# A two-layer hybrid decoder step: recurrence pace, place of the decode update, and how the output projections get their inputs

## The chip, the core and the metric

One NeuronCore of a Trainium2 chip runs the whole program. The engines work side by side, each through its own queue in order: TensorE (PE, with its weight loads PEld), VectorE (DVE), ScalarE (ACT), GpSimd (POOL) and SyncE (SP), which here only issues DMA transfers. The metric is the device time of one execution in microseconds; lower is better.

## The reference

The step takes 1024 new prompt tokens behind 16 meta tokens and 8 single decode tokens through two layers of width 1024. Layer 0 is a Conformer convolution and an MLP, layer 1 is RWKV-7 time mixing and an MLP. What matters here is layer 1:

```python
def _wkv7_step(S, inp):
    r_t, w_t, k_t, v_t, kk_t, a_t = inp
    sa = jnp.einsum('bhvk,bhk->bhv', S, -kk_t)
    S = (S * w_t[:, :, None, :] + sa[..., None] * (kk_t * a_t)[:, :, None, :]
         + v_t[..., None] * k_t[:, :, None, :])
    y = jnp.einsum('bhvk,bhk->bhv', S, r_t)
    return S, y
...
    kk = kk / jnp.maximum(jnp.sqrt(jnp.sum(kk * kk, axis=-1, keepdims=True)), L2_EPS)
...
    S_final, ys = lax.scan(_wkv7_step, S0.astype(f32), xs)
...
    out = ((yn + bonus).astype(h.dtype) * g) @ w_o
    return out, h[:, -1], S_final.astype(S0.dtype)

def _sqrelu_mlp(h, w_in, w_out):
    return jnp.square(jax.nn.relu(h @ w_in)) @ w_out
```

There are 16 heads of 64, the MLP is 4096 wide, and `yn` is the head-wise normalised `y`. The scan runs over 1040 prompt tokens; the decode tokens make one step each from a state of their own.

## The kernel before

**Groups, chunks and stages.** Features lie on the 128 partitions as 8 tiles (`KT`), tokens along the free dimension. Layer 0 runs over three groups of tokens. The time mixing (`mixer_in`) runs over four groups `G1` of 256 to 272 tokens: for each of 8 feature blocks p it projects r and v (8 matmuls each), and for the next group the keys (`keys`), and makes from them the operands `ab` of the recurrence, written to memory as `d_ab`. The recurrence works on 17 chunks: chunk 0 is the meta tokens, and each group gives four chunks of 64 tokens (group 0 gives chunks 0 to 4, and group 3 gives 13 to 16). The output projection (`mixer_out`, 24 matmuls for each of 8 output blocks) and the MLP of layer 1 run over three groups `G2` of 328 and 352 tokens: group 0 by itself, then groups 1 and 2 together. Their products are three matmuls each, of a high and a low part of weights and inputs (`split`, `load_w`); GpSimd makes the low parts of the weights (`wi_lo`, `wo_lo`).

**The recurrence.** A chunk needs the inverse of a triangular matrix for each head. `inverses` makes it for all chunks of a group at once on VectorE: 30 steps of two instructions (`tt`, `ni`), each needing the one before, then a store to `d_p`. `front(c)` loads a chunk's operands, makes the products `A` in two halves, masks them into `xa` and `nr`, and transposes the inverse `p32` in blocks into `x32`. `chunk(c)` goes on with the products gg (from x32), bT, W, po, U, S and Y in this order; the results pass through VectorE and ScalarE (`w1`, `p64`, `uv`, `fs`, `sv`). Chunk c+1 needs the state `sv` of chunk c.

**What sets the order.** TensorE executes the mixer and the first group's output projection and MLP in the order in which the program yields them (`manual_schedule`); a scheduler orders the other engines' instructions by when they could run and by program order. `recurrence` is a generator that yields a weight after each step (`RW`, 27.7 a chunk). In the mixer `tick` runs 7 times for a feature block or so: it makes a step of the inverse, gives the recurrence a credit of `PACE[g]` and lets it run until the credit is used. In the MLP of group 0 `fill`, made by `filler`, does the same at 208 points: over all of them it takes a stated weight from each of several streams, here the recurrence, the decode update and the normalisation of y (`norm_gate`, tiles ey, ems, eq, ez), whose result `d_z` is what the output projection reads.

**The decode update.** `decode_step` brings the decode operands into place through four transposes (`pdd`) and then updates the 8 x 16 decode states in 16 slices of 128x256 (`Sdec`, `t4`, printed as t in the profile): a load, nine VectorE instructions and a store each, with two buffers. The last normalisation unit waits for it.

**The output projection's inputs.** `mixer_out` loads each of the 8 input tiles `zr` by a transfer of its own into a three-deep scratch buffer, splits it into `z`, and loads and splits the weights `wo` of an output block where that block begins. The MLP's inputs `m_h` and `m_l` take the places of `z`, so they wait for the last reads of it; the products' sums of squares come from the matmul `st_m`.

Of the kernel before, what the change touches and what calls it, by code (L numbers as in the profile page):

```python
# [8 lines left out]
F32 = mybir.dt.float32  # L9
# [7 lines left out]
P = 128  # L17
D = 1024
KT = D // P
# [16 lines left out]
N2 = 352  # L36
# [12 lines left out]
def hybrid_step(tc, x_prompt, x_sample, state_conv, state_shift, state_wkv, meta_tokens,  # L49
# [8 lines left out]
    nc = tc.nc  # L58
    ctx = ExitStack()
    with ctx:  # L60
# [61 lines left out]

        def open_tmp(stack, nmax, tag, bufs=3, **kw):
            cur["n"] = cur["wide"] = nmax
            cur["tmp"] = pool(stack, f"tmp{tag}", bufs, **kw)
            cur["stat"] = pool(stack, f"stat{tag}", 1, **kw)

# [741 lines left out]
        def keys(g, fill):  # L869
# [10 lines left out]
            for p in range(KT):  # L880
                yield
                ps = proj(next(wrkv), act, n, nm("k", p), fill)
                k_ = kept[g, p] = pr.tile([P, N1], F32, name=nm("st", p), tag="st", bufs=KT + 1)
                nc.scalar.copy(k_[:, :n], ps[:, :n])
                sq = pr.tile([P, N1], F32, name=nm("sq", p), tag="rk", bufs=2)
                nc.scalar.activation(sq[:, :n], ps[:, :n], AF.Square, scale=vec("k_k", p))
                add_pn()
                add_pn = to_pn(p, sq)
            r16 = lorap.tile([P, N1], F32, name=nm("r16"), tag="lf")
            r16p = norm[g] = [lorap.tile([P, N1], F32R, name=nm("r16" + q), tag="r16" + q, bufs=2)[:, :n] for q in "hl"]  # L890
# [7 lines left out]
        def mixer_in(g, tick):  # L898
# [75 lines left out]
            act_v = mixed(3)  # L974
            r16p = norm.pop(g)
            ks = iter(())

# [54 lines left out]
            for p in range(KT):  # L1032
                both()
                ps = proj(next(wrkv), act, n, nm("r", p), both)
                rk2 = pr.tile([P, 2, N1], F32, name=nm("rk2", p), tag="rk2", bufs=2)
# [23 lines left out]
                pb = bank(nm("pb", p))  # L1059
                spread(pb[:, :n], r16p, p)  # L1060
                nc.vector.scalar_tensor_tensor(nkk[:, :n], kp[:, :n], nvec("k_k", p), pb[:, :n], op0=ALU.mult, op1=ALU.mult)
# [39 lines left out]
                if g < 3:  # L1101
                    if p == 0:
                        for _ in ranked(PP, prepare(g + 1)):
                            pass
                        ks = keys(g + 1, both)
                        next(ks)
                    for _ in keys_of(p):
                        next(ks, None)
# [49 lines left out]
        def front(c):  # L1158
# [10 lines left out]
            nc.sync.dma_start(p32, d_p[c].rearrange("k r t -> r k t"))  # L1169
            yield RW[0]  # L1170
            mask = lambda x: m_ar[:, x].unsqueeze(1).broadcast_to([P, 4, HS])
            for j in range(0, KT, 4):
# [14 lines left out]
                if j == 0:  # L1187
                    yield RW[1]
            x32 = w_([P, KT, 32], "x32", c)
            nc.vector.transpose(flat(x32), flat(p32))  # L1190
            chunks[c] = xa, bk, nr, no, p32, x32
# [262 lines left out]
        ng0 = norm_gates(GN_OF[0])  # L1454
        PACE = [0, 2.0, 2.0, 2.0]

# [7 lines left out]
        with in_order():  # L1464
            shift_in()
            for _ in prepare(0):
                pass
            for _ in keys(0, lambda: None):
                pass
            for g in range(4):  # L1470
                mixer_in(g, lambda slow=1.0: tick(g, slow))
            carry["tail"]()
            while invert():
                pass
            advance(CHUNK_WAIT * NCH, NEED[GN_OF[0][-1]])
            for _ in ng0:
                pass
        ld.close()


        with ExitStack() as l1:
            open_tmp(l1, N2, "2", 3)
            actp = pool(l1, "actp1", 1)
            open_weights(l1, 0, {"w": 5}, "f")
            residp = pool(l1, "resid1", 1)
# [6 lines left out]
            def mixer_out(g, residp, actp, fill, add):  # L1492
                lo, n = G2[g]
                h1 = hl[g] = residp.tile([P, KT, cur["wide"]], F32, name=f"h1_{g}", tag="h")
                nc.sync.dma_start(h1[:, :, :n], d_h[:, :, lo:lo + n])
                z = new_acts(actp, f"z{g}", cur["wide"])
                for p in range(KT):
                    t = tt(f"zr{g}{p}", "t1")
                    nc.sync.dma_start(t[:, :n], d_z[:, p, lo:lo + n])
                    split(z[0][p][:, :n], z[1][p][:, :n], t[:, :n], nc.vector)  # L1500
                for m in range(KT):
                    ps = dense(load_col(rwkv_w_o[0], m, f"wo{g}_{m}", nc.gpsimd), z, n, f"oo{g}_{m}", fill)
                    nc.vector.tensor_add(h1[:, m, :n], h1[:, m, :n], ps[:, :n])
                    add(m, h1[:, m, :n])
                    fill()
# [57 lines left out]
            def group(g, actp, hidp, sums):  # L1563
# [3 lines left out]


            ng2 = norm_gates(GN_OF[2])
            fill, rest = filler(2 * KT + MLP_POINTS,  # L1570
                                ([until(NCH - 1)], FA * CHUNK_WAIT * (NCH - 1 - st["done"])),
                                ([decode_step()], 82), ([norm_gates(GN_OF[1]), ng2], NGA))
            add, sums = sums_of(0)
# [63 lines left out]
```

## Time and profile before

| | |
|---|---|
| time, median of 3 runs | 2803.23 us (2798.64 to 2806.42) |
| the profiled execution: its own time | 2803.45 us |
| its span, first to last instruction | 2801.7 us |
| TensorE busy | 2654.4 us (95%) |
| VectorE, ScalarE, GpSimd busy | 63%, 41%, 53% |
| granted TensorE clock, mean | 0.977 |
| mixer from its second group on, MLP of group 0 up to its block 16 | 1310 to 1827.5 us, 1899.7 to 2097 us |

All times count from the span's start. A row of the windows view gives for a stretch the busy time and the number of instructions of each engine, then the granted clock, the DMA share and GB/s. A row of groups gives line, engine, operation, tiles and shapes with its count, then busy time and mean duration in ns, then the idle time before and what ended it. A row of waits gives who waited for whom, the total in us, how often, and the longest. A row of the timeline gives start and duration in us. Tile names stand without their numbers there.

### The profile page before, as it was taken

The numbers are of one execution on the slowest core, as the hardware profiler recorded it, in microseconds if no ns is written. First come the engines' busy times: TensorE is split into PE (matmuls) and PEld (weight loads), VectorE is DVE, ScalarE is ACT, GpSimd is POOL, SyncE is SP. The second block draws the span as 40 slices with busy tenths as digits, with TensorE's granted clock in tenths as the row PEclk, the third lists the DMA queues.
The fourth block names the chain that finished last, engine by engine and source line by source line (L and its number), as shares of the span: only waits on it lengthen the run. The fifth ranks groups of instructions, "written<-read, shape, count | busy, mean of one in ns | idle before, by whom it ended". The sixth has DMA issues, their size and how long they took to land. (4 is left out here: it accounts for less than half of the span.)

```text
span 2801.7 us, 51779 instructions
## 1 busy us (share of the span) xinstructions
PE 2654.4 (95%) x19866; PEld 2502.9 (89%) x19866; DVE 1772.9 (63%) x3550; ACT 1141.9 (41%) x2101; POOL 1497.7 (53%) x2066
## 2 busy tenths in 40 slices
PE   8998999999999999999998999978999999999998
PEld 7998999999999999787777778767889999999998
DVE  5999999996454544244756555589985554434444
ACT  5545444543354333233343443444444452222223
POOL 6676877887788866022111112366568763333332
PEclk9998999999999999999999999989999999999999
DMA  6663544454445553567778767877775642222211
GB/s 179 176 178 89 160 136 134 135 177 136 138 138 159 170 149 95 163 192 196 188 175 203 184 162 188 190 201 187 181 212 160 179 122 81 71 72 69 68 53 42
DMA packets 624599, 412.31 MB, mean 147 GB/s; under 512 B 121865, under 2 KB 567497, under 8 KB 624351
## 3 DMA queue, kind: packets, MB, share of 16 engines
q1 hardware_dynamic: 543436, 358.60, 45.1%
q10 hardware_dynamic: 72386, 24.56, 4.2%
q0 software_dynamic: 8528, 25.83, 2.8%
q8 instruction: 157, 2.57, 0.4%
q14 instruction: 92, 0.75, 0.1%
HBM read 345.76 MB, written 64.07 MB: 146 GB/s over the span
## 5 line engine op out<-in xcount | busy, mean ns | idle before, releaser
L161 POOL TENSOR_TENSOR wo_lo<-wo_raw,wo_hi 128x256 fp32r<-128x256 f32 x736 | 564.3, 798 | 261.0 <-ACT wo_hi L156 250.2
L161 POOL TENSOR_TENSOR wi_lo<-wi_raw,wi_hi 128x256 fp32r<-128x256 f32 x640 | 488.2, 794 | 282.7 <-ACT wi_hi L156 268.1
L186 PE MATMUL out<-hh,wo_hi 128*128 128x352 f32 (+2 forms) x1536 | 503.5, 328 | 21.5 <-DVE h L354 10.9
L354 DVE TENSOR_TENSOR h<-h,out 128x352 f32<-128x352 f32 (+2 forms) x768 | 387.5, 510 | 200.2 <-PE out L188 199.6
L188 PE MATMUL out<-hl,wo_hi 128*128 128x352 f32 (+2 forms) x1536 | 494.3, 324 | 5.5 <-DVE hl L140 5.5
L188 PE MATMUL ps_in<-m_l,wi_hi 128*128 128x352 f32 (+2 forms) x1536 | 495.5, 323 | 2.7 <-DVE m_l L284 2.6
L186 PE MATMUL ps_in<-m_h,wi_hi 128*128 128x352 f32 (+2 forms) x1536 | 496.4, 323 | 1.2 <-DVE h L354 1.2
L187 PE MATMUL out<-hh,wo_lo 128*128 128x352 f32 (+2 forms) x1536 | 495.8, 323 | 0.0
L187 PE MATMUL ps_in<-m_h,wi_lo 128*128 128x352 f32 (+2 forms) x1536 | 492.6, 321 | 0.0
L518 DVE SCALAR_TENSOR_TENSOR cv<-u,wdw,cv 128x352 f32<-128x352 f32 (+2 forms) x720 | 376.3, 571 | 0.7
L156 ACT CAST wi_hi<-wi_raw 128x1024 fp32r<-128x1024 f32 x160 | 168.0, 1050 | 399.9 <-PE out L188 195.8
L156 ACT CAST wo_hi<-wo_raw 128x1024 fp32r<-128x1024 f32 x184 | 192.6, 1049 | 320.0 <-PE out L188 159.0
L186 PEld LDWEIGHTS out<-hh,wo_hi 128*128 128x128 f32 x1536 | 293.1, 191 | 27.7 <-DVE h L354 13.2
L188 PEld LDWEIGHTS out<-hl,wo_hi 128*128 128x128 f32 x1536 | 291.1, 190 | 7.0 <-DVE hl L140 6.9
L186 PEld LDWEIGHTS ps_in<-m_h,wi_hi 128*128 128x128 f32 x1536 | 290.0, 189 | 3.9 <-issue 1.7
L187 PEld LDWEIGHTS out<-hh,wo_lo 128*128 128x128 f32 x1536 | 292.8, 191 | 0.6
L188 PEld LDWEIGHTS ps_in<-m_l,wi_hi 128*128 128x128 f32 x1536 | 288.6, 188 | 5.0 <-DVE m_l L284 4.1
L187 PEld LDWEIGHTS ps_in<-m_h,wi_lo 128*128 128x128 f32 x1536 | 289.4, 188 | 0.9
L341 DVE SCALAR_TENSOR_TENSOR r<-ps_in,rs_m 128x352 f32<-128x352 f32 (+2 forms) x192 | 98.3, 515 | 245.9 <-PE ps_in L188 240.7
L140 DVE TENSOR_TENSOR hl<-s,hh 128x352 fp32r<-128x352 f32 (+2 forms) x192 | 142.5, 743 | 104.6 <-ACT hh L139 104.4
L343 ACT ACTIVATE s<-r 128x352 f32<-128x352 f32 (+2 forms) x192 | 93.5, 490 | 121.9 <-DVE r L341 121.6
L1021 POOL DMA_DIRECT2D d_n<-n x32 | 24.4, 764 | 208.4 <-DVE n L1011 131.3
(354 smaller groups left out, 4855.9 us busy)
## 6 DMA issues: line engine op xcount, KB each, us to landing
wi_raw<-in_w_mlp_in_dram SPq DMA_DIRECT2D x160, 512.0 KB, 4.0
wo_raw<-in_w_mlp_out_dram SPq DMA_DIRECT2D x160, 512.0 KB, 3.8
wk_raw<-in_rwkv_w_k_dram SPq DMA_DIRECT2D x32, 512.0 KB, 7.2
wr_raw<-in_rwkv_w_r_dram SPq DMA_DIRECT2D x32, 512.0 KB, 4.2
wv_raw<-in_rwkv_w_v_dram SPq DMA_DIRECT2D x32, 512.0 KB, 4.5
d_ab<-ab POOLq DMA_DIRECT2D x32, 512.0 KB, 4.4
pg_raw<-in_conv_w_pw_dram SPq DMA_DIRECT2D x24, 512.0 KB, 6.8
pa_raw<-in_conv_w_pw_dram SPq DMA_DIRECT2D x24, 512.0 KB, 4.1
```

Source lines behind the costliest of these rows:

```text
L140: eng_lo.tensor_sub(lo, src, hi.bitcast(F32))
L156: nc.scalar.copy(hi[:, :a * b], raw[:, :a * b])
L161: eng_lo.tensor_sub(lo[:, cs], raw[:, cs], hi[:, cs].bitcast(F32))
L186: nc.tensor.matmul(ps, w[0], act[0], start=first, stop=False)
L187: nc.tensor.matmul(ps, w[1], act[0], start=False, stop=False)
L188: nc.tensor.matmul(ps, w[0], act[1], start=False, stop=last)
L341: nc.vector.scalar_tensor_tensor(r[:, :n], ps[:, :n], 0.0, rs()[:, :n], op0=ALU.max, op1=ALU.mult)
L343: nc.scalar.activation(s[:, :n], r[:, :n], AF.Square)
L354: nc.vector.tensor_add(hv[:, 4 * i + m, :], hv[:, 4 * i + m, :], ps[:, :n])
L518: nc.vector.scalar_tensor_tensor(acc[m][:, :n], ug[:, m, j:j + n], wdw[:, m, j:j + 1], acc[m][:, :n], op0=ALU.mult, op1=ALU.add)
L1021: nc.gpsimd.dma_start(d_n[ch0:ch0 + ncg, p].rearrange("c r t -> r c t"), n32[:, :ncg])
```

## The change

It has five parts. (1) `PACE` goes from 2.0 for every group to 1.4, 1.3 and 2.4, and four more ticks run after the last group. (2) The norm of a group's keys (the last matmul into `pn`, then `r16`) is done behind the first matmuls of the next group's first r projection (`first`, `carry["keys"]`). (3) `front` transposes the inverse before its products. (4) The decode stream begins with 74 empty steps and is stretched to 164 in all, so its first transposes come after 74/164 of the 208 points. (5) `mixer_out` loads two or three z tiles by one transfer into the weights' landing buffers (`cur["raw"]`) and each block's weights two blocks ahead; the pools `wsp` and `stat2` change places in the order of allocation.

```diff
-        def open_tmp(stack, nmax, tag, bufs=3, **kw):
+        def open_tmp(stack, nmax, tag, bufs=3, stats=True, **kw):
...
+            if stats:
+                cur["stat"] = pool(stack, f"stat{tag}", 1, **kw)
...
                 add_pn()
                 add_pn = to_pn(p, sq)
+            yield
             r16 = lorap.tile([P, N1], F32, name=nm("r16"), tag="lf")
...
-            r16p = norm.pop(g)
-            ks = iter(())
+            ks, kend = iter(()), carry["keys"]
+
+            def first():
+                both()
+                next(kend, None)
...
-                ps = proj(next(wrkv), act, n, nm("r", p), both)
+                ps = proj(next(wrkv), act, n, nm("r", p), both if p else first)
...
-                spread(pb[:, :n], r16p, p)
+                spread(pb[:, :n], norm[g], p)
...
-                        ks = keys(g + 1, both)
+                        ks = carry["keys"] = keys(g + 1, both)
...
             yield RW[0]
+            x32 = w_([P, KT, 32], "x32", c)
+            nc.vector.transpose(flat(x32), flat(p32))
...
-            x32 = w_([P, KT, 32], "x32", c)
-            nc.vector.transpose(flat(x32), flat(p32))
...
-        PACE = [0, 2.0, 2.0, 2.0]
+        PACE = [0, 1.4, 1.3, 2.4]
...
-            for _ in keys(0, lambda: None):
-                pass
+            carry["keys"] = keys(0, lambda: None)
+            for _ in range(KT + 1):
+                next(carry["keys"])
             for g in range(4):
                 mixer_in(g, lambda slow=1.0: tick(g, slow))
+            for _ in range(4):
+                tick(3, 1.0)
             carry["tail"]()
...
-            open_tmp(l1, N2, "2", 3)
+            open_tmp(l1, N2, "2", 3, False)
+            open_weights(l1, 0, {"w": 5}, "f")
             actp = pool(l1, "actp1", 1)
-            open_weights(l1, 0, {"w": 5}, "f")
+            cur["stat"] = pool(l1, "stat2", 1)
...
+                block = lambda m: load_col(rwkv_w_o[0], m, f"wo{g}_{m}", nc.gpsimd)
                 z = new_acts(actp, f"z{g}", cur["wide"])
-                for p in range(KT):
-                    t = tt(f"zr{g}{p}", "t1")
-                    nc.sync.dma_start(t[:, :n], d_z[:, p, lo:lo + n])
-                    split(z[0][p][:, :n], z[1][p][:, :n], t[:, :n], nc.vector)
+                ws, per = [], 8 * P // n
+                for p in range(0, KT, per):
+                    t = cur["raw"].tile([P, 8 * P], F32, name=f"zr{g}{p}", tag="raw")
+                    some = min(per, KT - p)
+                    v = t[:, :some * n].rearrange("p (k t) -> p k t", k=some)
+                    nc.sync.dma_start(v, d_z[:, p:p + some, lo:lo + n])
+                    if p == 0:
+                        ws.append(block(0))
+                    for i in range(some):
+                        split(z[0][p + i][:, :n], z[1][p + i][:, :n], v[:, i], nc.vector)
+                ws.append(block(1))
                 for m in range(KT):
-                    ps = dense(load_col(rwkv_w_o[0], m, f"wo{g}_{m}", nc.gpsimd), z, n, f"oo{g}_{m}", fill)
+                    if m + 2 < KT:
+                        ws.append(block(m + 2))
+                    ps = dense(ws.pop(0), z, n, f"oo{g}_{m}", fill)
...
+            DL, DN = 74, 90
+
+            def late_start(n):
+                for _ in range(n):
+                    yield 1
...
-                                ([decode_step()], 82), ([norm_gates(GN_OF[1]), ng2], NGA))
+                                ([late_start(DL), decode_step()], DL + DN), ([norm_gates(GN_OF[1]), ng2], NGA))
```

**TensorE, from the mixer's last block to the products gg of chunk 13.** pb3_7 to pk3_7 belong to group 3's last feature block, ps_oo0_m is output block m of group 0, and out1_0_0_3 is a block of the MLP's second product. Before:

```order
L755 MATMUL pb3_7_19441<-r16l3_17978,hspread_12511 128x264
L992 MATMUL vt3_7_19468<-ident_58,vv3_7_19407 128x128 x2
L1009 MATMUL nn3_7_19475<-ab3_7_19458 32x32 x16
L1025 MATMUL pk3_7_19494<-rk3_7_19456,hsum_12482 128x264
L186 MATMUL ps_oo0_0_19696<-z0_h0_19639,wo0_0_hi_19689 128x328
...
L1251 MATMUL W11_19709<-sv_12562,xa1_12567 64x64 x16
...
L1251 MATMUL W12_20232<-sv_12562,xa0_12566 64x64 x16
...
L188 MATMUL out1_0_0_3_20676<-hl10_0_20331,wo1_0_0_0_hi_20561 128x328
L1226 MATMUL gg13_20684<-x3213_20654,no13_20280 32x32 x16
```

In the changed kernel:

```order
L756 MATMUL pb3_7_19529<-r16l3_17744,hspread_12511 128x264
L1281 MATMUL S11_19554<-uv_12563,bkt11_19298 64x64 x16
L1288 MATMUL Y11_19571<-sv_12562,xa1_12567 64x64 x16
...
L1231 MATMUL gg12_19632<-x3212_19475,no12_19424 32x32 x16
...
L1014 MATMUL nn3_7_19677<-ab3_7_19546 32x32 x16
L1030 MATMUL pk3_7_19696<-rk3_7_19544,hsum_12482 128x264
...
L1256 MATMUL W12_19919<-sv_12562,xa0_12566 64x64 x16
...
L189 MATMUL ps_oo0_6_20313<-z0_l7_19856,wo0_6_hi_20150 128x328
L1231 MATMUL gg13_20341<-x3213_20113,no13_19967 32x32 x16
L1249 MATMUL bT130_20365<-ident_58,bk13_19962 128x128 x4
...
L187 MATMUL ps_oo0_7_20381<-z0_h0_19841,wo0_7_hi_20256 128x328
```

The recurrence leaves the mixer one chunk further on (W12 is next, not W11), part of that chunk stands ahead of nn3_7, and gg13 stands ahead of the last output block instead of in the MLP.

**VectorE, at the end of the last block inverse.** ni13 and tt13 are the inverse of chunks 13 to 16, x3213 is its transposition for chunk 13, and m10_l are the low parts of the MLP's input. Before:

```order
L1142 TENSOR_TENSOR ni13_19499<-ni13_19499,tt13_1_19588 128x30
L1503 TENSOR_TENSOR h1_0_19637<-h1_0_19637,ps_oo0_6_20163 128x328
L284 SCALAR_TENSOR_TENSOR m10_l0_20297<-h1_0_19637,pvec_84,m10_h0_20289 128x328
...
L284 SCALAR_TENSOR_TENSOR m10_l6_20303<-h1_0_19637,pvec_84,m10_h6_20295 128x328
L1190 STREAM_TRANSPOSE x3213_20654<-p3213_20281 128x256
L284 SCALAR_TENSOR_TENSOR m10_l7_20304<-h1_0_19637,pvec_84,m10_h7_20296 128x328
```

In the changed kernel:

```order
L1522 TENSOR_TENSOR h1_0_19839<-h1_0_19839,ps_oo0_6_20313 128x328
...
L1147 TENSOR_TENSOR ni13_19701<-ni13_19701,tt13_1_19790 128x30
L1177 STREAM_TRANSPOSE x3213_20113<-p3213_19968 128x256
L1243 TENSOR_SCALAR p6413_20361<-p3213_19968,par32q_12477 128x8x32 x2
L285 SCALAR_TENSOR_TENSOR m10_l0_20417<-h1_0_19839,pvec_84,m10_h0_20409 128x328
```

The transposition follows the inverse's last step directly, and all of m10_l comes after it.

**VectorE, in the MLP of group 0 from its block 20.** r1_j and hl10 make the hidden values, out1_9 adds the second product to h1_0, and Sdec, t4, sa and yd are the decode update. Before, where all 16 slices are done ahead of block 14:

```order
L341 SCALAR_TENSOR_TENSOR r1_20_0_23182<-ps_in1_20_0_23157,rs_m10_20378 128x328
L140 TENSOR_TENSOR hl10_20_23156<-s1_20_0_23184,hh10_20_23155 128x328
L341 SCALAR_TENSOR_TENSOR r1_21_0_23222<-ps_in1_21_0_23197,rs_m10_20378 128x328
L354 TENSOR_TENSOR h1_0_19637<-h1_0_19637,out1_9_0_0_23237 128x328
L354 TENSOR_TENSOR h1_0_19637<-h1_0_19637,out1_9_0_1_23245 128x328
L140 TENSOR_TENSOR hl10_20_23156<-s1_21_0_23224,hh10_20_23155 128x328
```

In the changed kernel:

```order
L342 SCALAR_TENSOR_TENSOR r1_20_0_23094<-ps_in1_20_0_23069,rs_m10_20498 128x328
L1384 TENSOR_TENSOR Sdec3_23157<-Sdec3_23157,t43_23158 128x256
L1385 TENSOR_TENSOR t43_23158<-dq_22802 128x256
L1386 TENSOR_TENSOR Sdec3_23157<-Sdec3_23157,t43_23158 128x256
L141 TENSOR_TENSOR hl10_20_23068<-s1_20_0_23096,hh10_20_23067 128x328
L1387 TENSOR_TENSOR t43_23158<-Sdec3_23157,dq_22802 128x256
L1388 TENSOR_REDUCE yd_22878<-t43_23158 128x4
L342 SCALAR_TENSOR_TENSOR r1_21_0_23134<-ps_in1_21_0_23109,rs_m10_20498 128x328
L1380 TENSOR_TENSOR t44_23220<-Sdec4_23219,dq_22802 128x256
L355 TENSOR_TENSOR h1_0_19839<-h1_0_19839,out1_9_0_0_23149 128x328
```

The decode update now stands among the MLP's own instructions, its first slice behind block 17 and its last one behind block 30; four instructions of a slice or so come between two of the MLP's.

More of the change, by code (lines that the diff above doesn't have):

```diff
@@ L121, in hybrid_step @@
         cur = {}
-        def open_tmp(stack, nmax, tag, bufs=3, **kw):
+        def open_tmp(stack, nmax, tag, bufs=3, stats=True, **kw):
             cur["n"] = cur["wide"] = nmax
             cur["tmp"] = pool(stack, f"tmp{tag}", bufs, **kw)
-            cur["stat"] = pool(stack, f"stat{tag}", 1, **kw)
+            if stats:
+                cur["stat"] = pool(stack, f"stat{tag}", 1, **kw)
         def stat(name, tag, bufs, w=None):
```

## The prediction

> **What bounds the kernel now.** I read the windows first, cut at the places where the change acts, then the waits of TensorE (PE) in each stage, then the groups of VectorE (DVE) and GpSimd (POOL) there. The profiled execution took 2803.45 us (span 2801.7 us); the median of the three runs, 2803.23 us, is the same to 0.01%, so the sum below is made against 2803.45. A difference of 0.3% (8.4 us) is about what a measurement of this kernel can tell from none.
>
> The stages, with busy time of each engine; PEclk is the granted clock as a share:
>
> ```profile
> core 0: us, PE busy (x) PEld busy (x) DVE busy (x) ACT busy (x) POOL busy (x), PEclk, DMA share, GB/s
> 1310.00:1827.50 517.50, 476.42 (x5211) 393.17 (x5210) 298.74 (x721) 210.35 (x539) 96.74 (x182) 0.97 0.74 187
> 1827.50:1899.70 72.20, 53.40 (x589) 48.27 (x590) 62.42 (x113) 32.86 (x61) 47.86 (x61) 0.86 0.70 193
> 1899.70:2097.00 197.30, 178.73 (x2026) 167.89 (x2024) 177.66 (x358) 86.68 (x164) 116.97 (x133) 0.96 0.74 194
> 2097.00:2204.00 107.00, 105.26 (x697) 104.54 (x698) 53.66 (x99) 44.29 (x64) 90.12 (x120) 1.00 0.51 157
> 2204.00:2290.00 86.00, 80.54 (x486) 78.23 (x485) 53.72 (x78) 49.71 (x91) 66.61 (x83) 0.98 0.58 171
> ```
>
> I call them M (mixer from its second group on), B (last block inverse, beside the output projection of group 0), C (MLP of group 0 with recurrence and decode update), D (the same MLP, blocks 17 to 31, with neither) and E (output projections of groups 1 and 2). PE is the bound in all: what counts is its idle time and the time at a low clock. M loses 517.5 - 476.4 = 41.1 us idle and at most 3% of 517.5 = 15.5 us to the clock. In B and C VectorE is busy for 86% and 90%, and PE waits for it. In D PE is full and VectorE half idle. The change moves work among M, B, C and D; PE's own work stays the same.
>
> **The change part by part.** *Pace (M).* At the mixer's end the recurrence stands one chunk further than before. What a chunk costs PE, from the stretch 1400 to 1827.5 (9 or 10 chunks: 32 instructions of W, U, S, po, gg and of each Y row a chunk, of A two halves):
>
> ```profile
> L1176 PE MATMUL A<-xa,bk 64*128 64x128 f32 x320 | 24.2, 292 | 0.0
> L1276 PE MATMUL S<-uv,bkt 128*64 128x64 f32 x320 | 13.5, 244 | 1.6 <-DVE uv L1268 1.4 <-ACT uv L1269 0.3
> L1267 PE MATMUL U<-w,p 64*64 64x64 f32 x320 | 12.1, 222 | 2.3 <-ACT p L1260 2.2
> L1283 PE MATMUL Y<-sv,xa 128*64 128x64 f32 x320 | 11.8, 229 | 0.0
> L1244 PE MATMUL bT<-ident,bk 128*128 128x128 f32 x80 | 11.3, 280 | 0.3 <-DVE nr L1186 0.3
> L1286 PE MATMUL Y<-uv,nr 128*64 128x64 f32 x320 | 11.1, 222 | 0.0
> L1251 PE MATMUL W<-sv,xa 128*64 128x64 f32 x288 | 10.4, 225 | 0.0
> L1226 PE MATMUL gg<-x,no 32*32 32x32 f32 x320 | 7.3, 193 | 0.0
> L1226 PE MATMUL po<-p,gg 32*32 32x32 f32 x288 | 6.2, 192 | 0.0
> ```
>
> That is 2.42 + 1.35 + 1.21 + 2.29 + 1.13 + 1.16 + 0.73 + 0.69 = 11.0 us, which M takes over: **+11**. Against it stands what an even pace saves. Before, four chunks are crowded into part of a group and the rest has none; a crowded and an emptier stretch read:
>
> ```profile
> 1500.00:1600.00 100.00, 89.64 (x932) 73.31 (x917) 63.71 (x157) 39.38 (x98) 15.50 (x24) 0.95 0.72 192
> 1700.00:1800.00 100.00, 98.17 (x994) 81.47 (x993) 58.21 (x148) 40.61 (x118) 28.36 (x67) 1.00 0.69 185
> ```
>
> and the largest waits of M are of this kind:
>
> ```profile
> PE pb L755 <- ACT vv L1054: 10.7, 6, 4.0
> PE nn L1009 <- DVE ab L1093: 3.2, 1, 3.2
> ```
>
> ScalarE copies chunk results (no, bkt, yt) ahead of the projection's vv. M now loses 56.6 us, 10.9%. At the emptier stretch's rate, 1.8% of 528 us, it would lose 10; at today's, all of it. I take 6%, 32 us, since the last group's pace rises from 2.0 to 2.4: **-25** (0 to -47). In it are the nn wait of 3.2 us, which the four added ticks fill with S11, Y11, A12 and gg12, and the key norm's last matmul, now behind three others. What a late norm would hold is pb, two projections later.
>
> *Block inverse (B).* Here the price is not in the diff. PE must run gg13 (32 matmuls on x32 of chunk 13) before the last output block; before, it stood in the MLP's fourth block. The chain up to x32:
>
> ```profile
> 1827.48 0.46 PE L1009 MATMUL nn<-ab 64*32 64x32 f32 x32 [3.21 <-DVE ab L1093]
> 1834.52 0.64 PE L186 MATMUL ps_oo<-z_h,wo_hi 128*128 128x328 f32 x1 [5.79 <-ACT wo_hi L156]
> L1141 DVE TENSOR_TENSOR tt<-ni x30: 192/561/1129, 1836.9 to 1888.5; 128x30 f32<-128x30 f32 x2, 128x58 f32<-128x58 f32 x2, 128x84 f32<-128x84 f32 x2, 128x108 f32<-128x108 f32 x2
> 1837.00:1889.80 52.80, 42.67 (x469) 40.07 (x469) 50.48 (x95) 19.45 (x35) 36.50 (x47) 0.89 0.70 187
> 1893.28 0.37 SPq L1169 DMA_DIRECT2D p<-d_p  x1
> 1898.32 0.43 DVE L1190 STREAM_TRANSPOSE x<-p 128x256 f32<-128x256 f32 x1
> L284 DVE SCALAR_TENSOR_TENSOR m_l<-h,pvec,m_h 128x328 fp32r<-128x328 f32 x8 | 7.8, 1015 | 0.7 <-ACT m_h L283 0.7
> 1899.50 1.27 PE L237 MATMUL st_m<-acc_m,ones_d 128*128 128x328 f32 x4
> 1827.50:1837.00 9.50, 3.54 (x41) 2.58 (x42) 2.98 (x8) 5.70 (x10) 4.50 (x7) 0.54 0.72 241
> ```
>
> From the last nn to the transposition pass 70.8 us: the store and load of n, 60 inverse steps on a VectorE busy for 50.5 of 52.8 us, then the store and load of p. The change leaves these 60 steps and about as many others among them, so x32 comes 70.8 us after nn again. PE has less to do until then (one chunk less) and stands at gg13. Behind it, in order, come gg13 and bT13 (1.9 us), the first third of the last output block (24 matmuls at 105.26/697 = 0.15 us, 1.2 us), whose reads free the tiles of the eight m_l (7.8 us, done before under the same wait, now behind it), then st_m: 70.8 + 1.9 + 1.2 + 7.8 + about 1.3 for the hand-overs = 83 us against 72.0: **+11** (4 to 14). The 5.79 us wait for the first output weights, which the landing buffers and earlier weight loads shorten, lies inside these 71 us and gains nothing while the inverse ends later. After the two waits of 3.2 and 5.8 us the clock is 0.54 in the last row. The Trainium skill ("TensorE: Matmul & The Clock Gate", What's actually happening) says that an idle window of about 3.4 us halves the clock; this trace agrees, and by it the restart behind gg13 would cost an estimated 1.7 us more.
>
> *Decode update taken out of C.* C idles 18.6 us and loses up to 7.9 us to the clock, mostly for VectorE:
>
> ```profile
> PE bT L1244 <- DVE nr L1186: 7.3, 5, 3.2
> PE gg L1226 <- DVE nr L1186: 2.7, 1, 2.7
> ```
>
> With the decode gone VectorE is under two thirds busy there. I keep 5 us of waits, three times D's 1.7, for the chunk's chain W, U, S; of the clock loss 6 count, some falling into idle time. The earlier transposition of p takes 0.43 us out from between nr and gg and is in this. By st_m the recurrence also has 11.0 - 1.16 - 0.69 = 9.1 us more behind it. So 18.6 + 6 - 5 + 9.1: **-29** (-20 to -36).
>
> *Decode update put into D.*
>
> ```profile
> 1899.70:2097.00 197.30, 66.45 (x128) 0.96 0.74 194
> L1377 DVE TENSOR_TENSOR Sdec<-Sdec,dq 128x256 f32<-128x256 f32 x16 | 9.2, 572 | 0.0
> L1376 DVE TENSOR_REDUCE sa<-t 128x4 f32<-128x256 f32 x16 | 6.6, 414 | 0.3
> L140 DVE TENSOR_TENSOR hl<-s,hh 128x328 fp32r<-128x328 f32 x17 | 13.0, 771 | 3.4 <-ACT hh L139 3.4
> L140 DVE TENSOR_TENSOR hl<-s,hh 128x328 fp32r<-128x328 f32 x14 | 12.1, 863 | 8.7 <-ACT hh L139 8.7
> ```
>
> The first row is the decode's tile t alone (128 operations), with L1377 the whole update: 75.7 us, 144 operations. The order puts all of them between the blocks 17 and 30, that is into D, where VectorE has 53.7 us of its own: 129.4 us in a stretch that PE needs 107 us for. The split of the next group's first inputs (z_l) comes forward by about 4 us, overlapping starts save as much. VectorE becomes the bound: **+22**. At 0.41 us an operation, the reduction's price, it would be 59 + 53.7 - 107 = +6; the other end is the first rival's. Queued behind each decode operation are r, hl and the h sums; PE waits for them through its banks. The 32 decode transfers move with it on SP's queue, between weight loads.
>
> *Landing buffers (E).* 24 loads become 11, weights come two blocks early. Group 2's first matmuls waited
>
> ```profile
> PE ps_oo L188 <- DVE z_l L140: 3.4, 3, 2.2
> ```
>
> and 5.5 us were idle in E: **-3** (0 to -5). The other allocation order of pools costs nothing that this trace shows.
>
> Sum: 11 - 25 + 11 - 29 + 22 - 3 = -13, so 2803.45 - 13 = 2790.5 us.
>
> **The rivals.** *First, D is bound by two engines that shut each other out; slower.* POOL splits weights in D for 90.8 us:
>
> ```profile
> L161 POOL TENSOR_TENSOR wo_lo<-wo_raw,wo_hi 128x256 fp32r<-128x256 f32 x72 | 55.5, 802 | 10.0 <-ACT wo_hi L156 9.9
> L161 POOL TENSOR_TENSOR wi_lo<-wi_raw,wi_hi 128x256 fp32r<-128x256 f32 x48 | 35.3, 767 | 8.2 <-ACT wi_hi L156 8.2
> L161 POOL TENSOR_TENSOR wi_lo<-wi_raw,wi_hi 128x256 fp32r<-128x256 f32 x64 | 55.9, 905 | 46.8 <-ACT wi_hi L156 33.4 <-issue 12.6 <-POOL sw L1257 0.6
> ```
>
> Each is slower where the other is dense: wi_lo 905 ns in C (VectorE 90%), 767 in D; hl 863 ns in D (POOL 84%), 771 in C (59%). The Trainium skill ("SBUF — State Buffer", Who interferes with whom) says that a VectorE instruction with two SBUF inputs and a GpSimd one that reads SBUF exclude each other, while a reduction does not take part; these rows lean that way. If they exclude each other wholly, D takes 90.8 + (75.7 - 32 x 0.41) + 12.1 = 165 us, +58 instead of +22: 2826. Halfway to my 129, at 147, it is 2808.5. It turns slower than before by 0.3% from D = 151 us on. Against it: C holds 117 us of POOL beside 178 of VectorE in 197. I price it at 2815, chance 0.22.
>
> *Second, the even pace only spreads the losses*: recurrence now also runs at the group borders, which were empty and are dense with mixing. M then gains 6 instead of 25: 2809.5, or 2806 with a cheaper B. Chance 0.18.
>
> *Third, both terms fall well*: M falls to 22 us of loss (-35), D to +12 because the decode runs near its shortest durations: 2770. Chance 0.17.
>
> **How the numbers follow.** Forecast 0.43, from 2778 to 2803: faster 0.33, same 0.10. First rival: slower 0.18, same 0.04. Second: same 0.12, slower 0.06. Third: faster 0.17. Together faster 0.50, same 0.26, slower 0.24. The range of 2764 to 2820 takes in the third rival and the first up to D = 159; outside lie their far ends.
>
> **What would show it.** Right: the time from the last nn to st_m grows to about 83 us with PE standing before gg13; C's idle time falls to 5 us; D takes about 129 us with VectorE near full; M idles less than 30 us. Wrong: gg13 without a wait (B is then a gain of its own), D near 107 us (the decode fits), or M idle as before. A D above 150 us is the first rival.

## The result and the profile after

The changed kernel takes 2784.03 us (median of nine runs, 2773.99 to 2795.94) against 2803.23 us, a ratio of 0.9941 with a 95% interval of 0.9925 to 0.9958. The forecast was 2790.5 us. The profiled execution of the changed kernel was the slowest of its nine: 2795.94 us, span 2794.2 us; a second profile of the same kernel, below among the experiments, has a span of 2784.8 us.

The stages are cut here at instructions that both kernels have, so C and D differ a little from the prediction's cuts: M from the first group's last nn to the last nn, B to the sums of squares st_m, C to block 18 of the MLP, D to the end of that MLP, E to the st_m of the next two groups. First the windows of before in these cuts, then those of after (stretch, its length, busy time of PE, PEld, DVE, ACT, POOL with instructions, granted clock, DMA share, GB/s):

```profile
1307.30:1827.50 520.20, 479.12 (x5257) 395.47 (x5257) 299.71 (x725) 211.12 (x542) 98.36 (x184) 0.97 0.75 187
1827.50:1899.50 72.00, 53.20 (x589) 48.08 (x590) 62.42 (x113) 32.66 (x61) 47.86 (x61) 0.86 0.70 193
1899.50:2103.10 203.60, 183.29 (x2052) 171.72 (x2051) 183.60 (x368) 90.39 (x173) 123.07 (x139) 0.96 0.73 194
2103.10:2215.40 112.30, 110.28 (x722) 109.74 (x723) 56.37 (x105) 47.49 (x70) 89.71 (x121) 0.98 0.54 162
2215.40:2286.20 70.80, 67.36 (x421) 66.44 (x419) 41.98 (x59) 41.20 (x74) 59.06 (x74) 1.00 0.57 169
```

```profile
1308.10:1821.30 513.20, 484.24 (x5519) 404.14 (x5518) 312.50 (x741) 213.04 (x551) 108.19 (x195) 0.97 0.77 191
1821.30:1901.40 80.10, 55.65 (x519) 51.08 (x519) 57.51 (x115) 30.88 (x58) 41.58 (x53) 0.77 0.69 185
1901.40:2078.20 176.80, 169.34 (x1858) 160.84 (x1857) 115.04 (x210) 87.04 (x164) 110.16 (x138) 0.98 0.70 191
2078.20:2211.70 133.50, 117.93 (x727) 113.73 (x728) 125.55 (x253) 51.29 (x76) 102.94 (x123) 0.95 0.57 168
2211.70:2277.10 65.40, 65.40 (x417) 65.38 (x415) 35.91 (x50) 38.33 (x68) 54.30 (x70) 1.00 0.63 175
```

The five stages changed by -7.0, +8.1, -26.8, +21.2 and -5.4 us: -9.9 us. The head, which is layer 0 and the first group's mixing up to its last nn, came out 0.8 us longer, the rest behind E 1.6 us.

In B, TensorE stands where the prediction said. From the timeline of the changed kernel, PE and DVE (start, duration, engine, line, operation, in brackets the idle time before it):

```profile
1888.86 0.45 DVE L1177 STREAM_TRANSPOSE x<-p 128x256 f32<-128x256 f32 x1 [6.83 <-DMA p<-d_p]
...
1889.45 1.06 PE L1231 MATMUL gg<-x,no 32*32 32x32 f32 x32 [15.82 <-DVE x L1177]
...
1892.48 0.47 PE L188 MATMUL ps_oo<-z_h,wo_lo 128*128 128x328 f32 x1
1892.75 0.47 PE L189 MATMUL ps_oo<-z_l,wo_hi 128*128 128x328 f32 x1
...
1895.72 0.31 PE L188 MATMUL ps_oo<-z_h,wo_lo 128*128 128x328 f32 x1
1895.87 0.31 PE L189 MATMUL ps_oo<-z_l,wo_hi 128*128 128x328 f32 x1
...
1901.41 1.27 PE L238 MATMUL st_m<-acc_m,ones_d 128*128 128x328 f32 x4
```

gg13 waits 15.8 us for the inverse's transposition (13.6 us in the second profile), and only 12 us later comes st_m. In D, VectorE is busy for 94%. PE's largest waits there (who waited for whom, total, times, longest):

```profile
PE out L187 <- DVE r L342: 7.3, 5, 1.8
PE out L187 <- ACT hh L140: 6.7, 1, 6.7
```

The first row is waits for VectorE. The second is one wait at D's end, for the last block's hidden values:

```profile
2198.67 0.49 DVE L342 SCALAR_TENSOR_TENSOR r<-ps_in,rs_m 128x328 f32<-128x328 f32 x1
...
2198.69 1.04 ACT L157 CAST wo_hi<-wo_raw 128x1024 fp32r<-128x1024 f32 x1 [2.95 <-DMA wo_raw<-in_rwkv_w_o_dram]
...
2201.49 0.47 ACT L344 ACTIVATE s<-r 128x328 f32<-128x328 f32 x1
...
2202.51 0.64 PE L187 MATMUL out<-hh,wo_hi 128*128 128x328 f32 x1 [6.69 <-ACT hh L140]
```

VectorE makes r only after splits of the next group's inputs and the first two steps of the last normalisation unit, which reads the decode's last result; ScalarE makes s only after two casts of the next group's weights, the first of which waits for its load. In before this wait is 1.6 us, with the landing buffers alone 3.9, in the changed kernel without them 4.2.

The groups of VectorE and GpSimd around D, in the changed kernel:

```profile
L1385 DVE TENSOR_TENSOR t<-dq 128x256 f32<-128x256 f32 x16 | 11.4, 709 | 0.2
L1383 DVE TENSOR_TENSOR t<-sa,dq 128x256 f32<-128x256 f32 x16 | 11.3, 708 | 0.0
...
L141 DVE TENSOR_TENSOR hl<-s,hh 128x328 fp32r<-128x328 f32 x16 | 10.6, 660 | 1.5 <-ACT hh L140 1.5
...
L1382 DVE TENSOR_TENSOR Sdec<-Sdec,dq 128x256 f32<-128x256 f32 x16 | 10.0, 628 | 0.0
...
L1388 DVE TENSOR_REDUCE yd<-t 128x4 f32<-128x256 f32 x16 | 6.6, 412 | 0.2
...
L162 POOL TENSOR_TENSOR wi_lo<-wi_raw,wi_hi 128x256 fp32r<-128x256 f32 x48 | 40.3, 870 | 8.2 <-ACT wi_hi L157 8.2
```

The decode's operations with two inputs take 0.54 to 0.71 us here, by all of their rows (0.49 to 0.60 in before's C), its reductions 0.41 us as before, and GpSimd's wi_lo 870 ns (767 in before's D).

### The profile page after: what moved, and what is told of

It is laid out like the page before. It is cut to its first block, busy times and chain, and to the rows that moved or that the text cites. A ratio compares the mean times of both kernels' runs of the same rounds, so it can differ in the third digit from the quotient of the medians.

```text
span 2794.2 us, 51683 instructions
## 1 busy us (share of the span) xinstructions
PE 2653.8 (95%) x19866; PEld 2506.4 (90%) x19866; DVE 1783.2 (64%) x3550; ACT 1138.5 (41%) x2097; POOL 1498.1 (54%) x2066
## 5 line engine op out<-in xcount | busy, mean ns | idle before, releaser
L187 PE MATMUL out<-hh,wo_hi 128*128 128x352 f32 (+2 forms) x1536 | 505.3, 329 | 31.5 <-DVE r L342 15.6
```

The costliest lines, as they stand in the source:

```text
L187: nc.tensor.matmul(ps, w[0], act[0], start=first, stop=False)
```

## The experiments

Ratios are to the kernel before, each with its 95% interval. The stage lengths in us, cut as above, one profiled execution each:

| kernel | ratio | M | B | C | D | E |
|---|---|---|---|---|---|---|
| before | 1 | 520.2 | 72.0 | 203.6 | 112.3 | 70.8 |
| changed, first profile | 0.9941 (0.9925 to 0.9958) | 513.2 | 80.1 | 176.8 | 133.5 | 65.4 |
| changed, second profile | 0.9937 (0.9922 to 0.9952) | 512.2 | 79.7 | 174.9 | 132.4 | 65.4 |
| decode in its old place | 0.9971 (0.9959 to 0.9982) | 513.0 | 81.0 | 199.2 | 115.6 | 67.0 |
| old pace, no ticks | 0.9969 (0.9957 to 0.9981) | 518.5 | 69.9 | 183.9 | 132.9 | 65.4 |
| without landing buffers | 0.9943 (0.9929 to 0.9957) | 512.6 | 81.4 | 174.6 | 131.1 | 67.6 |
| before + landing buffers | 1.0001 (0.9992 to 1.0010) | 523.0 | 71.4 | 201.9 | 115.1 | 67.1 |
| before + key norm, transposition | 0.9986 (0.9978 to 0.9995) | 518.6 | 70.8 | 206.6 | 112.6 | 72.0 |
| gg13 later | 0.9901 (0.9888 to 0.9915) | 510.2 | 70.6 | 175.0 | 132.5 | 65.4 |
| gg13 later, two thirds of the decode in C | 0.9905 (0.9891 to 0.9919) | 512.4 | 69.4 | 189.4 | 122.1 | 65.5 |
| gg13 later, a quarter in C | 0.9893 (0.9880 to 0.9907) | 512.2 | 69.6 | 177.8 | 130.2 | 65.4 |

M of before and of before with the landing buffers is the same code and differs by 2.8 us, so a difference of 3 us in one stage says nothing by itself.

### The changed kernel again

> The changed kernel once more, unaltered, for a second profile and a time beside the variants of this set. The profiled execution of it at first had the lowest granted clock (0.972) and the longest time of its nine. Expected: ratio 0.994 (0.9925 to 0.9955); a span near 2783 us with the same stages to about 2 us each (M 513, B 80, C 177, D 133, E 65), the difference to the first profile lying in the head (layer 0) and in the clock of all stages. Rival: the scatter sits in one stage, say D, whose length then differs by 5 us or more.

The ratio was 0.9937, the span 2784.8 us. The head took 1301.1 us against 1308.1, the stages agree to 2 us, and the granted clock was 0.976 against 0.972. So the first profile's delay is spread, most of it over the head: 4.1 us in layer 0, which no part of the change touches, and 2.9 us in the first group's mixing. Over all profiles here layer 0 (up to the mixing's first product, pss) took 1127.8 to 1134.0 us. Single profiles are therefore compared below by their stages, and whole kernels by the ratio.

### The decode in its old place

```diff
-                                ([late_start(DL), decode_step()], DL + DN), ...
+                                ([decode_step()], 82), ...
```

> The changed kernel with the decode update back in its old place (from the first filler point on). Times as a ratio to the kernel before, measured beside it; the changed kernel stands at 0.9941. Theory of the prediction: D (block 18 of the MLP to its end) gets back to about 111 us from 133, and C (from the products' sums of squares to block 18) keeps only the 9 us of recurrence done earlier and goes from 177 to about 195: -22 + 18 = -4 us against the changed kernel, ratio 0.9926 (0.990 to 0.996). So the late place of the decode is worth nothing by itself. Rival: taking the decode out of C is what brought the gain; without it the time rises by 10 us or more, ratio 0.9977 or above.

It measured 0.9971: the late decode is worth 0.3%, and the theory's -4 us is refuted; the rival's bound of 0.9977 lies inside the interval. Its windows of C and D:

```profile
1897.40:2096.60 199.20, 176.11 (x1853) 166.01 (x1851) 177.68 (x352) 86.70 (x161) 117.73 (x137) 0.95 0.69 188
2096.60:2212.20 115.60, 111.59 (x722) 111.22 (x723) 58.33 (x111) 50.02 (x74) 92.71 (x124) 0.97 0.56 160
```

Against the two profiles of the changed kernel C is 22 to 24 us longer and D 17 to 18 us shorter. I had taken D at before's 111 us, but with landing buffers it is 115 us, and had believed that C keeps 9 us from the pace; C in this kernel is only 4.4 us shorter than before.

### The old pace

```diff
-        PACE = [0, 1.4, 1.3, 2.4]
+        PACE = [0, 2.0, 2.0, 2.0]
...
-            for _ in range(4):
-                tick(3, 1.0)
```

> The changed kernel with the pace 2.0, 2.0, 2.0 of before and without the four added ticks. Theory of the prediction, with the sizes that the trace of the changed kernel shows: the mixer gets the 7 us back that it saved (+7; +14 by the prediction's own sizes), TensorE no longer stands at the block inverse (-8), and the recurrence has a chunk more behind it in C (+9): +8 us against the changed kernel, ratio 0.997 (0.995 to 0.999). Rival: the pace only pushes a chunk into a place where TensorE then waits 15.8 us for it, and is worth nothing or less: ratio 0.994 or below.

It measured 0.9969, as the theory had it. The windows of M and B, to be read beside the first two of the changed kernel:

```profile
1306.20:1824.70 518.50, 475.85 (x5259) 394.27 (x5259) 303.34 (x725) 215.43 (x545) 101.78 (x189) 0.97 0.75 186
1824.70:1894.60 69.90, 54.76 (x582) 49.41 (x583) 57.64 (x116) 31.26 (x58) 46.86 (x57) 0.84 0.73 206
```

The pace takes 13.7 us of idle time out of M (42.7 to 29.0), puts 8.4 us of work into it (475.9 to 484.2), lengthens B by 10 us and shortens C by 7 to 9 us.

### gg13 behind independent work

```diff
             xa, bk, nr, no, p32, x32 = chunks.pop(c)
+            if c == NCH - 4:
+                yield 12.0
...
-                                ([until(NCH - 1)], FA * CHUNK_WAIT * (NCH - 1 - st["done"])),
+                                ([until(NCH - 1)], FA * CHUNK_WAIT * (NCH - 1 - st["done"]) + 12.0),
```

> The changed kernel with gg13, the first product that needs the last block inverse, put 12 weight units later, from before the last output block to behind the first product of the MLP's first output block; the recurrence runs on at the same rate behind it. Theory: the 15.8 us in which TensorE stands at gg13 are pure loss, since the output blocks and the first MLP blocks do not need the inverse; the sums of squares st_m then come 64 to 68 us after the last nn instead of 80, and the whole is 12 to 16 us shorter: ratio 0.989 (0.987 to 0.991). Rival: the chain of the inverse on VectorE, the output blocks' additions and the weights hold st_m anyway, or the chunks that end later push into D: a gain under 4 us, ratio 0.993 or above.

It measured 0.9901, inside the theory's range, and B is 9.1 to 9.5 us shorter than in the changed kernel, at 70.6 us where 64 to 68 were expected: not all of the 15.8 us came back. Its window of B:

```profile
1814.90:1885.50 70.60, 53.16 (x479) 47.86 (x479) 60.55 (x114) 28.52 (x54) 41.91 (x53) 0.84 0.78 204
```

and PE's largest waits there:

```profile
PE ps_in L189 <- DVE m_l L285: 5.3, 2, 2.7
PE Y L1290 <- DVE nr L1193: 3.1, 1, 3.1
PE ps_oo L189 <- DVE z_l L141: 3.0, 3, 1.8
PE ps_in L187 <- ACT m_h L284: 2.4, 1, 2.4
```

gg13 is no longer among them; the MLP's inputs m_h and m_l take the rest. Its work cost nothing further back: C is as long as in the changed kernel. The stand at gg13 was a loss that the change brought with it, and a later place for gg13 removes it.

### The landing buffers by themselves, and left out

> The kernel before with the fifth part of the change alone (input tiles by landing buffers, output weights two blocks ahead, order of the pools). Theory of the prediction: the 5.8 us wait at the first output block goes, but lies inside the time of the block inverse; only E gains, 3 to 5 us: ratio 0.9985 (0.997 to 1.000). Rival: in the kernel before nothing in B stands for the inverse, since gg13 comes in the fourth MLP block; then the 5.8 us count as well and it gains 9 to 11 us: ratio 0.9965 or below.

> The changed kernel without its fifth part (each input tile by its own transfer, output weights loaded where their block begins, old order of the pools). By itself that part moved the kernel before by nothing (ratio 1.0001): the wait for the first output weights became a longer one for the first input tile, and E's gain was given back in D. Theory: in the changed kernel it is worth as little in B, where gg13 is waited for anyway, and E against D come out at 2 us or less: ratio 0.994 to 0.9955 (the changed kernel 0.9937). Rival: with VectorE full at D's end the splits of E's inputs come late without the wide loads, and E has 5 us more of waits: ratio 0.996 or above.

Alone they gave 1.0001, outside the range of theory and rival alike, and the changed kernel without them 0.9943, as its theory had it: they are worth nothing that can be measured. The timeline of PE with the landing buffers alone, at the start of B:

```profile
1842.95 0.64 PE L187 MATMUL ps_oo<-z_h,wo_hi 128*128 128x328 f32 x1 [7.32 <-ACT z_h L140]
```

The weights are there, and the first matmul now waits 7.3 us for the first input tile instead of 5.8 us for the weights. E becomes 3.7 us shorter and D 2.8 us longer, 2.3 of them in the wait at D's end (3.9 us against 1.6). In the changed kernel without them PE waits in B:

```profile
PE gg L1230 <- DVE x L1176: 14.8, 1, 14.8
PE S L1280 <- ACT uv L1273: 4.4, 1, 4.4
PE ps_oo L186 <- ACT wo_hi L156: 4.2, 1, 4.2
```

The wait for the weights is back, 4.2 us, and B is 81.4 us against 79.7 to 80.1: most of it is taken out of the time before gg13, which cannot come sooner.

### Key norm and transposition alone

> The kernel before with parts two and three alone: the norm of the keys behind the first matmuls of the next group, and the inverse transposed ahead of the products. Theory: the run with the old pace had a mixer 2 us shorter than before, and with the decode in its old place C was 4.5 us shorter than before with one chunk less, so these two parts give M -2 and C up to -2: ratio 0.9986 (0.997 to 1.000). Rival: they give the 4 us that the pace does not explain in C and more in M: ratio 0.997 or below.

0.9986, as expected in the whole, but not by the stages: M is 1.6 us shorter, C 3.0 us longer. That the early transposition helps C is not shown. What this run gained lies ahead of M, in the first group's mixing from pss to its last nn; before, then this run:

```profile
1131.20:1307.30 176.10, 172.00 (x1009) 141.45 (x1009) 63.40 (x145) 58.69 (x164) 33.01 (x64) 0.99 0.65 189
1127.80:1300.30 172.50, 169.39 (x1007) 140.01 (x1010) 60.79 (x142) 57.77 (x162) 32.65 (x64) 1.00 0.65 191
```

The eleven profiles of kernels with the key norm moved have 172.4 to 175.7 us there, the two of kernels without it 176.1 and 177.0. So this part seems to be worth up to about 3.6 us, in a place that the stages leave out; two waits of PE for the norm's squares, 1.0 us together in before, are gone.

### More of the decode back in C

```diff
-            DL, DN = 74, 90
+            DL, DN = 20, 90
```

> As the run with gg13 put later, and the decode update begins after 20 of 110 steps instead of 74 of 164: its slices start about the MLP's block 9 instead of 17 and run to block 29, half in C and half in D. Theory (VectorE bounds D, C has room: 116 us busy of 175): D falls from 132.5 to about 117 us, C rises by about 5 us: -10 us against the run with gg13 put later, ratio 0.9865 (0.985 to 0.988). Rival: C gets back as much as D gives, since each VectorE operation in C stands in the way of the recurrence's chain; before against early decode it was 22 us of C against 18 us of D: then no gain, ratio 0.989 to 0.991.

> The same with the decode beginning after 45 of 135 steps: slices from about block 14 on, a quarter of them in C. Theory: D about 124 us, C up by 2: -6 us against the run with gg13 put later, ratio 0.988 (0.9865 to 0.9895), between that run and the one with half of the decode in C. Rival as there: no gain, ratio 0.989 to 0.991.

With `DL` at 20, 11 of the 16 slices begin in C, not half as expected. The ratio is 0.9905, no gain: D falls by 10.4 us against the run with gg13 later, C rises by 14.4. The rival was right on that, but the recurrence's chain is only part of it: TensorE's idle time in C rises from 4.3 to 14.2 us, 6.1 us of it in waits for the MLP's r (2.6 with gg13 later alone) and 1.1 to 3.4 us each in waits for the recurrence's w, nr and fs, and its busy time rises by 4.5 us at a clock of 0.96 against 0.98. By these waits VectorE's idle time in C is there on average, not at the moments when its results are due. With a quarter in C (`DL` 45) the ratio is 0.9893, inside the ranges of theory and rival alike, and it can't be told from 0.9901; C +2.8, D -2.3 where about -8 was expected. A last variant put gg13 8 units later instead of 12, with the decode as in the second of these:

> The run with the decode from about block 14 on, with gg13 put 8 weight units later instead of 12: into the MLP's third block. Theory: x32 is there at about 70 us after the last nn and gg13 then comes at about 76 us, so nothing waits, and the recurrence ends 1 us sooner: ratio 0.989 (0.9875 to 0.9905), no difference that can be measured to the run with 12 units (0.9893). Rival: gg13 waits again by 2 us or more in the third block: ratio 0.991 or above.

0.9903 (0.9886 to 0.9920): no difference, and no wait of gg13. The versions with gg13 later all beat both kernels, by about 1% against before and 0.3 to 0.5% against the changed one; among them nothing is told apart.

### D without GpSimd's low parts

```diff
+            if eng_lo is nc.scalar:
+                nc.scalar.copy(lo[:, :a * b], raw[:, :a * b])
+                return v(hi), v(lo)
...
+            def eng_of(j):
+                return nc.scalar if layer and len(groups) == 1 and j >= 18 else eng_w
...
```

> The changed kernel, with the low parts of the MLP's weights from block 18 of group 0 on made by a copy on ScalarE instead of a subtraction on GpSimd; it leaves the subtraction of the high part out there, and GpSimd stands nearly still in D. Theory (the first rival's mechanism at part of its size): the decode's operations with two inputs in SBUF take 0.41 to 0.55 us when GpSimd is idle and up to 0.95 us when it runs; without it all of them fall to about 0.45 us, VectorE's time in D from 125.6 to about 105 us, and D from 133.5 to about 115 us. Rival (plain VectorE time bounds D, GpSimd plays no part): the durations stay at 0.55 to 0.71 us and D at 128 us or more; or ScalarE's added copies, some 30 us, hold TensorE instead, with waits for wi or wo from ScalarE in the list of waits.

There is one execution, of 2772.79 us, 16 us under the changed kernel's 2788.73 us (median) beside it. Its M, B, C and E are 510.9, 79.8, 174.8 and 65.4 us, within 2.3 us of the changed kernel's. Its window of D:

```profile
2072.30:2189.10 116.80, 112.26 (x728) 111.55 (x727) 104.17 (x253) 75.77 (x102) 13.27 (x17) 0.97 0.66 189
```

and the groups of VectorE around it (the decode's line numbers are 7 higher here):

```profile
L141 DVE TENSOR_TENSOR hl<-s,hh 128x328 fp32r<-128x328 f32 x16 | 8.4, 527 | 1.1 <-ACT hh L140 1.1
...
L1392 DVE TENSOR_TENSOR t<-dq 128x256 f32<-128x256 f32 x16 | 6.7, 422 | 0.2
...
L1390 DVE TENSOR_TENSOR t<-sa,dq 128x256 f32<-128x256 f32 x16 | 6.7, 419 | 0.0
L1388 DVE TENSOR_REDUCE sa<-t 128x4 f32<-128x256 f32 x16 | 6.7, 417 | 0.3
L1389 DVE TENSOR_TENSOR Sdec<-Sdec,dq 128x256 f32<-128x256 f32 x16 | 6.7, 416 | 0.0
```

and PE's largest waits in D:

```profile
PE out L191 <- ACT hh L140: 3.4, 1, 3.4
PE out L193 <- DVE hl L141: 1.1, 1, 1.1
```

The same 253 VectorE instructions take 104 us instead of 125.6, and D 116.8 instead of 133.5. The decode's two-input operations, the rows shown and the rest, fall to 0.42 to 0.45 us; the reduction stays. PE waits nowhere for the weights that ScalarE now makes, so the second rival falls too. So 16.7 of the 21.2 us by which D had grown go away with GpSimd's work, and are not VectorE's work as such.

## Why the prediction was right

**The whole.** The time lies 6.5 us under the forecast and inside its own range of 2778 to 2803. The forecast's sum was -13; the stages give -9.9 in the first profile and -14.3 in the second. That agreement is partly luck: M fell short, the landing buffers by themselves gave nothing, and the sum has no term for the first group's mixing, where the moved key norm seems to have gained up to 3.6 us.

**M: the direction right, the size too large.** Predicted -14, measured -7.0 and -8.0. The idle time is 29.0 us, under 30 as said, and the wait of the last nn is gone. The term that was mis-sized is "6%, 32 us" of loss, a saving of 25: it assumed that the clock recovers with the idle time. The mean stayed 0.97, so by the prediction's own reckoning 29.0 + 15 = 44 us are still lost, 12 fewer than before. The chunk cost 8.4 us against the run with the old pace, not 11: the times of the groups add up to more than the busy time, because matmuls overlap (in the rows of B above they take 0.31 us and begin 0.15 us apart).

**B: the stand right, the way behind it right in length by luck.** Predicted was a stand before gg13 and 83 us; there are 15.8 us and 80.1. The transposition came 67.6 us after the last nn where I had 70.8. Behind it the sum had 12.2 us and the trace has 12.0, but of other terms. The sum let st_m wait for the eight m_l (7.8 us); PE waited for none of them. It was busy throughout: 2.6 us for gg13 and bT13, 5.3 for the whole last output block, 4.1 for the MLP's first block. That the landing buffers gain nothing in B was right, but in the kernel before it was for another reason, the first input tile. The stand also cost clock: up to 1895.5 us the output block's matmuls began 0.27 us apart at a granted clock of 0.50, behind that 0.15 us apart, which makes about 1.6 us over twelve of them. The trace agrees there with the Trainium skill's halving after an idle window ("TensorE: Matmul & The Clock Gate", What's actually happening).

**C: right.** Predicted -29, measured -26.8. The runs split it into 22 to 24 us for the decode (19.6 in the sum) and 7 to 9 us for the chunk (9.1), together a little more than the whole.

**D: the number right, its reason half.** Predicted +22, measured +21.2. I priced the decode at its durations in C, 75.7 us, as work of VectorE. Those rows already held part of GpSimd's share. In D they grew to 85 us, and only because neighbouring instructions overlap did VectorE stay at 125.6 us. PE's share of D's growth is 13.6 us of idle time (2.0 to 15.6) and 7.7 us of busy time for as many matmuls (110.3 to 117.9, at a clock of 0.95 against 0.98); 6.7 us of the idle time are the one wait at D's end, for which the sum had no term. Without GpSimd's work D is 4.5 us longer than before, close to the low bound of +6 that 0.41 us an operation gave, and only 1.2 us longer than with the decode in its old place and the same landing buffers (115.6). So the first rival had the mechanism, and the forecast its size: 133.5 us is below the 151 from which it would have decided. The Trainium skill ("SBUF — State Buffer", Who interferes with whom) calls the shared ports an exclusive lock; with whole instructions shutting each other out, I had D near 165 us. That counted durations that GpSimd had already lengthened; by the shortest of this trace (112 operations of 0.41 us, 14 hl of 0.48, 121 subtractions of 0.72) it would be about 140 us, an estimate. D stayed under both. The trace agrees on who takes part, not on whole instructions: some operations that GpSimd covered for over three quarters took 0.41 us all the same.

**E: wrong in what it credits.** Predicted -3 for the landing buffers, and E shows -5.4, of which 3.2 are there without them (67.6 us). The failed step is that E was costed alone: loads that leave E enter D, and alone the part gives 1.0001.

**The rivals.** The second, a pace that only spreads its losses, is refuted: without the new pace the kernel is slower by 0.3%, though M's saving lies between the rival's 6 and the forecast's 25. The third needed a D of +12 and an M of -35; neither came.

## What to carry to other kernels

Work pushed forward in an in-order queue carries along the first instruction that needs a late result; find that instruction, and put independent work in front of it, or it takes back what the push gained (15.8 us here, of which a later place returned 9). Judge a place for two-input VectorE work by what GpSimd does there, not by VectorE's idle share alone. And cost an edit over the neighbouring stages too: what left E turned up in D.

## What the runs showed of the hardware

Whether GpSimd runs is visible operation by operation. VectorE and GpSimd in the changed kernel's D:

```profile
2128.81 0.41 DVE L1382 TENSOR_TENSOR Sdec<-Sdec,dq 128x256 f32<-128x256 f32 x1
...
2129.55 0.93 DVE L1383 TENSOR_TENSOR t<-sa,dq 128x256 f32<-128x256 f32 x1
...
2132.27 0.85 DVE L1386 TENSOR_TENSOR Sdec<-Sdec,t 128x256 f32<-128x256 f32 x1
...
2134.11 0.42 DVE L1388 TENSOR_REDUCE yd<-t 128x4 f32<-128x256 f32 x1
...
2129.47 3.37 POOL L162 TENSOR_TENSOR wi_lo<-wi_raw,wi_hi 128x256 fp32r<-128x256 f32 x4 [0.71 <-ACT wi_hi L157]
2133.06 3.22 POOL L162 TENSOR_TENSOR wi_lo<-wi_raw,wi_hi 128x256 fp32r<-128x256 f32 x4 [0.23 <-ACT wi_hi L157]
```

In GpSimd's gap before 2129.47 an operation takes 0.41 us, beside its subtractions 0.93 and 0.85, and the reduction 0.42 all the same. Of the decode's 111 two-input operations that overlap D, 13 beside which GpSimd ran for less than a tenth of the time took 0.41 to 0.43 us, and 77 that it covered for over three quarters 0.41 to 0.96, 0.68 in the mean. The additions h, with one input in PSUM, took 0.48 us in both cases. I had not expected the effect to be this sharp, nor that it would be most of D's price.
